# A decode stage woven into a feed-forward block: a value step of its own, and dense products handed out in halves

## The chip, the cores and the metric

The kernel runs on one core of a Trainium2 chip. The metric is the device time of one execution in microseconds (us); the kernel before was run three times, and the median counts. Beside these there is one profiled execution, whose instructions, waits and transfers can be looked at one by one.

## The reference

One layer of a hybrid decoder serves two groups of tokens with the same weights: a prompt of 512 tokens and a sample group of 8 sequences with 4 new tokens each, whose 4096 past tokens lie in a paged cache. Cut to its skeleton:

```python
h = h + 0.5 * rmsnorm(swiglu(rmsnorm(h, g0), wg[0], wu[0], wd[0]), g1)   # first FFN, 1024 -> 2816 -> 1024
m = mixer(rmsnorm(h, g2), ...)     # 4 HGRN2 heads (gated recurrence) and 4 MLA heads
h = h + rmsnorm(m, g3)
h = h + 0.5 * rmsnorm(swiglu(rmsnorm(h, g4), wg[1], wu[1], wd[1]), g5)   # second FFN

# MLA heads, latent form; for the sample group the keys are the cached ones and the new ones
past_c = cache_kv_latent[page_table].reshape(8, 4096, 256)
past_r = cache_k_rope[page_table].reshape(8, 4096, 64)
s = (einsum('bqhr,bsr->bhqs', q_lat, keys_c) + einsum('bqhd,bsd->bhqs', q_rope, keys_r)) / sqrt(192)
o_lat = einsum('bhqs,bsr->bqhr', softmax(masked(s)), keys_c)
```

All inputs and outputs are float32. Outputs are the new activations, the new latent rows and rotary keys, and the recurrent states.

## The kernel before

The 544 tokens are split in two parts: `a` with 256 prompt tokens and `b` with 256 prompt tokens and the 32 sample tokens. Activations lie transposed, features on the 128 partitions and tokens along the free dimension. A float32 product is made of three products of a high and a low part: `weight` (L214) loads a weight tile by a DMA on SyncE's queue into `wraw` (three buffers), casts it to its high part `wh` on ScalarE (L231) and subtracts for the low part `wl` on VectorE (L232); `gemm` (L243, matmuls recorded at L240) and `gemm_q` (L250, L258) multiply. `gemm_q` is a generator that yields behind every second block of 128 features.

The kernel is written as generators that are advanced in turn, and the order in which they are advanced is the order of priority; a scheduler then orders each engine's instructions, keeping to that order as far as its own estimate finds operands ready. So the source gives the order of the work nearly, not to the instruction.

The change is about the decode stage, which lies between the attention over the prompt and the second FFN of part `b`. Two streams share it:

- **Dense:** `gb = ffn(1, 5, (0,), u4, ...)` (L979), the second FFN of part `a`. Its 22 gate-and-up tiles come in chunks of 6, 6, 5 and 5. A tile is 24 products with the gate weights and 24 with the up weights (each 128x128 by 128x256), and behind them on VectorE `sil` times the rms factor (L311), a sigmoid on ScalarE (L287 to L289), two products (L313, L314) and a split into `hha` and `hla` (L154, L155). Behind each chunk stand 8 down columns of 18 or 15 products, added up in `ma` (L329, L331). A tile is one step of the generator, a down column too: 54 steps.
- **Decode:** `decode()` (L1131). The 8 sequences' caches are worked on as 16 halves. For each half `gather` (L1041) fetches two blocks of latent rows (1 MB each) and two of rotary keys by indirect DMAs on GpSimd's queue; the latent blocks go to six slots in turn (`ulb`, `uhb`, `ha`, `hb`, `mb`, `q0`), so that a gathering waits for the value products of three halves earlier. `turn` (L1060) transposes the rows to `kh` on VectorE (L1065, L1066; two buffers, so that it waits for the scores of the half before). `score` (L1069) makes 80 small matmuls of 64x32 weights (L1078), in two bursts of 40, and takes their maxima (`mxd`, `mxh`, L1085 to L1087). `peak` (L1089) spreads the maximum over the partitions with TensorE (L1091) and VectorE (L1093, L1096). `weigh` (L1098) takes exponentials on ScalarE (L1101). `place` (L1103) transposes them and copies them to `pbuf` on VectorE and ScalarE (L1105, L1109). `value` (L1111) makes 16 matmuls of 128x32 weights by 256 columns (L1117), and for every second half `gathered` (L1123) turns the sum (L1128, L1129).

`decode()` counts steps of a third of a half. With `at(k)` for the half that began k halves ago, a third with r = 0 is two steps: the first score burst, then the second burst together with the value products of the half before and the gather of a new half. r = 1 is one step, peak and the turning of the next half; r = 2 is one step, gathered and weigh, and place goes with the step after it. That is 79 steps in all. The loop that advances the two streams keeps them in proportion:

```python
na, nb = NS + (NS + 2) // 3, int((22 + 32) * DRATE)     # 79 decode steps, 43 dense steps
ia, ib = 1, 0
while ia < na:
    if ia * nb <= ib * na:
        next(ga, None)        # a decode step
        next(gn, None)        # scores of the new tokens, a few steps
        ia += 1
    else:
        next(gb, None)        # a dense step
        ib += 1
```

`decode_end` (L1170) combines the parts (`pb`, L1183). What is left of `gb` is handed out by `fill` (L1301) while the output projection and the second FFN of part `b` begin: `FILL` gives the numbers of steps.

Of the kernel before, what the change touches and what calls it, by code (L numbers as in the profile page):

```python
# [49 lines left out]
W0 = 0  # L50
JOBS = (0, 1, 2, 6, 7, 8, 3, 4, 5)
CQ, NST = (0, 0, 0, 3, 1), 3
FILL = (4, (7, 8, 9), (1, 2, 3, 4), 4)
PTB, PEB, QNB = 2, 3, 1
LEP, LXP, EB, XB = (), (), 2, 2
PAT = (2, 2, 2, 2, 2, 2, 2, 2, 2, 2, 1, 1, 1, 2, 3, 2)
PATL = (2, 2, 1, 1, 2, 1, 2, 1, 2, 2, 1, 1, 1, 2, 2, 1)
NW, WX = 2, 2
DRATE = 0.8
KHB = 2  # L60
LEVELS = (64, 32, 16, 8, 4, 2, 1)

# [37 lines left out]
def hybrid_step_kernel(  # L100
# [27 lines left out]
    def ps(name, tag="ps"):  # L128
        return pp.tile([P, 512], F32, name=name, tag=tag, bufs=NPS[tag])
# [30 lines left out]
    def sumsq(srcs, eng=None):  # L160
        n = srcs[0].shape[-1]
        acc = tmp("ssq", n)
        for k, s in enumerate(srcs):
            if k == 0:
                nc.scalar.activation(acc, s, AF.Square)
            else:
                q = tmp("sq1", n)
                nc.scalar.activation(q, s, AF.Square)
                (eng or nc.vector).tensor_tensor(acc, acc, q, op=ALU.add)
        return allsum(acc)  # L170
# [7 lines left out]
    def rstd(out, ss, n, r=None):  # L178
        t = tmp("rs_t", out.shape[-1])
        if r is None:  # L180
            nc.scalar.activation(t, ss, AF.Ln, scale=1.0 / n, bias=epst)
            nc.scalar.activation(out, t, AF.Exp, scale=-0.5)
        else:
            nc.vector.tensor_tensor(t, r, r, op=ALU.mult)
            nc.vector.scalar_tensor_tensor(t, ss, 1.0 / n, t, op0=ALU.mult, op1=ALU.mult)
            nc.scalar.activation(t, t, AF.Ln, scale=1.0, bias=epst)
            nc.scalar.activation(t, t, AF.Exp, scale=-0.5)
            nc.vector.tensor_tensor(out, t, r, op=ALU.mult)
# [19 lines left out]
    def rstd_u(u, x):  # L208
        rstd(u[2], sumsq([h[x][:, k] for k in range(KD)]), D)
# [25 lines left out]
    def mm3(out, pairs):  # L235
        n = 0
        last = 3 * len(pairs) - 1
        for (ah, al), (bh, bl) in pairs:
            for a, b in ((ah, bh), (ah, bl), (al, bh)):
                nc.tensor.matmul(out, a, b, start=n == 0, stop=n == last)  # L240
                n += 1

    def gemm(wt, act_):  # L243
        wh, wl, kt = wt
        acc = ps("acc", "acc")
        n = act_[0].shape[-1]
        mm3(acc[:, :n], [((wh[:, k], wl[:, k]), (act_[0][:, k], act_[1][:, k])) for k in range(kt)])
        return acc[:, :n]

    def gemm_q(wt, act_):  # L250
        wh, wl, kt = wt
        acc = ps("acc", "acc")
        n = act_[0].shape[-1]
        for k in range(kt):
            if k and k % 2 == 0:
                yield
            for i, (a, b) in enumerate(((wh, act_[0]), (wh, act_[1]), (wl, act_[0]))):
                nc.tensor.matmul(acc[:, :n], a[:, k], b[:, k], start=k + i == 0, stop=k == kt - 1 and i == 2)  # L258
        return acc[:, :n]
# [28 lines left out]
        nc.scalar.activation(out, out, AF.Ln, bias=ones[:, :1])  # L288
        nc.scalar.activation(out, out, AF.Exp, scale=-1.0)  # L289

    def ffn(i, n_post, xs, u, nxt=None, mid=None, late=None, fin=None, pre=()):
        pool = cur[-1]
        yield
        r2 = {x: u[x][2] for x in xs}
        mT = {x: actslot("m", x) for x in xs}
        ends = []
        for c, (f0, nf) in enumerate(FCH[i]):
            hh = {x: mk([P, FCH[i][0][1], HS[x]], F32R, "hh" + "ab"[x], pool=pool) for x in xs}
            hl = {x: mk([P, FCH[i][0][1], HS[x]], F32R, "hl" + "ab"[x], pool=pool) for x in xs}
            for j in range(nf):  # L300
                f = f0 + j
                wg_ = (w0 or [weight([wcols(w_g[i], 0, KD, f * P)], KD)]).pop(0)
                ga = {x: gemm(wg_, u[x]) for x in xs}
                wu_ = (w0 or [weight([wcols(w_u[i], 0, KD, f * P)], KD)]).pop(0)
                up = {x: gemm(wu_, u[x]) for x in xs}
                if late and f == 0:
                    late()
                for x in xs:
                    s = tmp("sil", HS[x], 3, pool)
                    t = tmp("sit", HS[x], 2, pool)  # L310
                    nc.vector.tensor_tensor(s, ga[x], r2[x], op=ALU.mult)  # L311
                    sigmoid(t, s)
                    nc.vector.tensor_tensor(s, s, t, op=ALU.mult)  # L313
                    nc.vector.tensor_tensor(s, s, up[x], op=ALU.mult)  # L314
                    split(hh[x][:, j], hl[x][:, j], s)
                yield
            last = c == len(FCH[i]) - 1
            if fin and c == BEG:
                fin.begin(u[xs[0]][2])
            if last:  # L320
                sacc = {x: tmp("ssm" + "ab"[x], HS[x], 1, pool) for x in xs}
            groups = [(d,) for d in range(KD)] if not last or len(xs) == 1 else [(d,) for d in range(KD - STAG)] + [tuple(range(KD - STAG, KD))]
            for grp in groups:
                wts = {d: pre.pop(0) if pre else weight([wcols(w_d[i], f0, nf, d * P)], nf, len(grp) > 1) for d in grp}
                for x in xs:
                    for d in grp:
                        acc = gemm(wts[d], (hh[x], hl[x]))
                        if c == 0:
                            nc.scalar.copy(mT[x][:, d], acc)  # L329
                        else:  # L330
                            nc.vector.tensor_tensor(mT[x][:, d], mT[x][:, d], acc, op=ALU.add)  # L331
                        if last:
                            sq = scale_sq(sacc[x], mT[x], d, gq, n_post, bool(fin) and d == KD - 1)
                        if last and fin and d >= LAG:
                            fin.column(mT[x], d - LAG)
                    if last and grp is groups[-1] and fin:
                        for d in range(KD - LAG, KD):
                            fin.column(mT[x], d)
                        fin.end(sacc[x], sq)
                    elif last and grp is groups[-1]:  # L340
                        ends.append(post(x, mT[x], sacc[x], u[x][2], nxt))
                        next(ends[-1])
                yield
        if mid:
            mid()
        for p in ends:
            for _ in p:
                pass
# [100 lines left out]
    u4 = {}  # L449
# [43 lines left out]
    with scope("mix") as mx_:  # L493
# [234 lines left out]
        with scope("hg"):  # L728
# [9 lines left out]
            for hd in range(NH):  # L738
                nx = hs_[hd + 1][0]() if hd + 1 < NH else some(CQ[hd])
                step = 0  # L740
# [235 lines left out]
    ffa = ExitStack()  # L976
    wx.append(ffa.enter_context(scope("ffa")))
    seam = []
    gb = ffn(1, 5, (0,), u4, late=lambda: rstd_u(u4[0], 0), pre=seam)  # L979
    next(gb)  # L980

    with scope("dec"):
# [48 lines left out]
        NS = 3 * NH2 + 11  # L1031
# [99 lines left out]
        def decode():  # L1131
            H = {}
            for t in range(NS):
                n, r = divmod(t, 3)

                def at(k):
                    return H.get(n - k)

                if n < NH2 and r == 0:
                    H[n] = Half(n)  # L1140
                if r == 0:
                    if at(2):
                        at(2).score(range(5))
                    if n < 3 and at(0):
                        at(0).gather()
                    yield
                    if at(2):
                        at(2).score(range(5, 10))
                    if at(3):
                        at(3).value(H.get(n - 4))  # L1150
                    if n >= 3 and at(0):
                        at(0).gather()
                    yield
                elif r == 1:
                    if at(2):
                        at(2).peak()
                    if at(1):
                        at(1).turn()
                    yield
                else:  # L1160
                    if at(3):
                        at(3).gathered()
                    if at(2):
                        at(2).weigh()
                    yield
                    if at(2):
                        at(2).place()
                H.pop(n - 5, None)
# [36 lines left out]

        ga, gn = decode(), decode_new()
        next(ga)
        na, nb = NS + (NS + 2) // 3, int((22 + 32) * DRATE)
        ia, ib = 1, 0
        while ia < na:  # L1210
            if ia * nb <= ib * na:
# [82 lines left out]
    with scope("fin"):  # L1294
# [22 lines left out]
        next(gp)  # L1317
        fill(FILL[0])
        hm = homes()
        f0, nf = FCH[1][-1]  # L1320
        for d, _ in enumerate(gp):
            if d in FILL[1]:
                fill(1)
            if d in FILL[2]:
                seam.append(weight([wcols(w_d[1], f0, nf, (len(seam) + 1) * P)], nf, home=next(hm)))
        fill(FILL[3])
        next(gB)
# [53 lines left out]
```

## Time and profile before

| | |
|---|---|
| three runs | 1341.04, 1342.49, 1344.46 us, median 1342.49 |
| profiled execution | 1339.38 us, span of its instructions 1337.6 us |
| mean granted TensorE clock | 0.991 |
| instructions | 29702 |
| read from and written to HBM | 181.48 MB and 9.67 MB, 143 GB/s over the span |

The profiled execution's own time is 1.8 us more than the span of its instructions. In the rows that follow, times are microseconds from the span's start; `PE` is TensorE's matmuls and `PEld` its weight loads, `DVE` VectorE, `ACT` ScalarE, `POOL` GpSimd, `SP` SyncE; L1078 is a line of the kernel; `out<-in` names the tiles, with buffer numbers left out; `x48` counts instructions, and a float32 matmul of the source is two rows in the trace. A matmul's duration is modelled and overlaps the next one's, so that the distance between starts tells more than the busy time. A chain of waits goes back from the last instruction, at each step to what released it; "issue" in it is time in which an engine waited for nothing that the profile shows.

### The profile page before, as it was taken

To read this page: it belongs to the slowest core of one execution; us is meant where nothing else is said; L and a number is where in the kernel's file an instruction comes from. 1 tells how busy PE (TensorE), PEld (TensorE's weight loads), DVE (VectorE), ACT (ScalarE), POOL (GpSimd) and SP (SyncE) were. 2 spreads that over 40 slices of the span, in tenths; PEclk is the share of its full clock that TensorE was granted. 3 is DMA by queue.
4 is the path that set the end of the run, shared out by engine and by line. 5 is a ranking of instruction groups with operands and counts; after the bars stand their busy time and mean duration, and the time that the engine had idled before them with its cause. 6 is when DMAs were issued, how large, how long until landed. Compare 5 with 4: busy or idle time off the path is not lost.

```text
span 1337.6 us, 29702 instructions
## 1 busy us (share of the span) xinstructions
PE 1292.3 (97%) x12316; PEld 1221.4 (91%) x12316; DVE 899.3 (67%) x1778; ACT 703.0 (53%) x1430; POOL 75.1 (6%) x79
## 2 busy tenths in 40 slices
PE   7999999999999999999999889999899999999997
PEld 6999999999999999999897787886788999999996
DVE  7553244444458788775867678998888868566664
ACT  6543244224456745454748654653455677554454
POOL 0000000000000000000000212322310000000000
PEclk9999999999999999999999989999999999999998
DMA  6233323232344222233232866977868555556452
GB/s 194 84 87 88 90 85 91 81 97 80 89 117 149 87 64 82 80 82 108 76 101 70 301 200 208 321 258 259 279 212 290 163 151 161 172 157 178 142 168 69
DMA packets 280309, 193.08 MB, mean 144 GB/s; under 512 B 12525, under 2 KB 271054, under 8 KB 275310
## 3 DMA queue, kind: packets, MB, share of 16 engines
q1 hardware_dynamic: 271968, 148.14, 37.9%
q0 software_dynamic: 7168, 41.95, 8.3%
q8 instruction: 97, 1.59, 0.5%
q10 hardware_dynamic: 1038, 1.09, 0.3%
q14 instruction: 38, 0.31, 0.1%
HBM read 181.48 MB, written 9.67 MB: 143 GB/s over the span
## 4 chain that ended last, share of the span: by engine, by line
PE 79%; DVE 11%; ACT 4%; DMA 4%; issue 2%; ACTq 0%; SPq 0%; DVEq 0%
PE acc L240 57%; PE acc L258 9%; DVE kh L1065 3%; DVE wl L232 2%; PE s L1078 2%; PE pa L643 2%; ACT wh L231 1%; DMA wraw<-w_u 1%; PE s L881 1%; PE o L1117 1%; PE pr L175 1%; DMA wraw<-w_g 1%; ACT pbuf L1109 1%; PE zx L544 1%; PE pS L716 1%
## 5 line engine op out<-in xcount | busy, mean ns | idle before, releaser
L231 ACT CAST wh<-wraw 128x1024 fp32r<-128x1024 f32 (+3 forms) x255 | 248.7, 977 | 339.7 <-PE acc L240 273.6
L232 DVE TENSOR_TENSOR wl<-wraw,wh 128x1024 fp32r<-128x1024 f32 (+3 forms) x255 | 288.6, 1133 | 141.3 <-ACT wh L231 140.8
L240 PE MATMUL acc<-uhb,wh 128*128 128x288 f32 x768 | 227.3, 296 | 0.8 <-ACT uhb L191 0.8
L240 PE MATMUL acc<-ulb,wh 128*128 128x288 f32 x768 | 227.0, 296 | 0.0
L240 PE MATMUL acc<-uhb,wl 128*128 128x288 f32 x768 | 225.6, 294 | 0.6 <-DVE wl L232 0.6
L240 PE MATMUL acc<-uha,wh 128*128 128x256 f32 x768 | 220.1, 287 | 5.5 <-DVE sil L311 5.3
L240 PE MATMUL acc<-ula,wh 128*128 128x256 f32 x768 | 217.5, 283 | 1.2 <-DVE ula L192 1.2
L240 PE MATMUL acc<-uha,wl 128*128 128x256 f32 x768 | 216.9, 283 | 0.4 <-DVE wl L232 0.2
L240 PEld LDWEIGHTS acc<-uha,wh 128*128 128x128 f32 x768 | 145.7, 190 | 9.5 <-DVE sil L311 5.7
L240 PEld LDWEIGHTS acc<-ula,wh 128*128 128x128 f32 x768 | 145.6, 190 | 1.7 <-DVE ula L192 1.6
L240 PEld LDWEIGHTS acc<-uha,wl 128*128 128x128 f32 x768 | 145.3, 190 | 1.0 <-DVE wl L232 1.0
L240 PEld LDWEIGHTS acc<-uhb,wh 128*128 128x128 f32 x768 | 144.1, 188 | 1.5 <-ACT uhb L191 1.0
L240 PEld LDWEIGHTS acc<-uhb,wl 128*128 128x128 f32 x768 | 144.4, 188 | 0.8 <-DVE wl L232 0.8
L240 PEld LDWEIGHTS acc<-ulb,wh 128*128 128x128 f32 x768 | 144.1, 188 | 0.1
L240 PE MATMUL acc<-hlb,wh 128*128 128x288 f32 x317 | 93.7, 296 | 0.0
L240 PE MATMUL acc<-hhb,wh 128*128 128x288 f32 x317 | 93.7, 297 | 0.0
L240 PE MATMUL acc<-hhb,wl 128*128 128x288 f32 x317 | 92.9, 294 | 0.0
L240 PE MATMUL acc<-hha,wh 128*128 128x256 f32 x297 | 87.0, 293 | 2.7 <-ACT hha L154 2.7
L240 PE MATMUL acc<-hla,wh 128*128 128x256 f32 x297 | 84.3, 284 | 1.1 <-DVE hla L155 1.1
L240 PE MATMUL acc<-hha,wl 128*128 128x256 f32 x297 | 84.3, 284 | 0.0
L314 DVE TENSOR_TENSOR sil<-sil,acc 128x256 f32<-128x256 f32 (+1 forms) x88 | 38.3, 436 | 49.4 <-PE acc L240 47.0
L313 DVE TENSOR_TENSOR sil<-sil,sit 128x256 f32<-128x256 f32 (+1 forms) x88 | 38.5, 440 | 43.2 <-ACT sit L289 42.9
(466 smaller groups left out, 2825.8 us busy)
## 6 DMA issues: line engine op xcount, KB each, us to landing
wraw<-w_g SPq DMA_DIRECT2D x66, 512.0 KB, 4.1
wraw<-w_u SPq DMA_DIRECT2D x66, 512.0 KB, 3.9
wraw<-w_in SPq DMA_DIRECT2D x24, 512.0 KB, 3.9
wraw<-w_d SPq DMA_DIRECT2D x32, 384.0 KB, 3.5
wraw<-w_d SPq DMA_DIRECT2D x32, 320.0 KB, 3.2
wraw<-w_o SPq DMA_DIRECT2D x16, 512.0 KB, 3.7
wraw<-w_d SPq DMA_DIRECT2D x16, 448.0 KB, 3.5
wraw<-w_d SPq DMA_DIRECT2D x8, 512.0 KB, 3.8
```

What stands on the lines that cost most here:

```text
L175: nc.tensor.matmul(pr[:, :n], ones, acc, start=True, stop=True)
L231: nc.scalar.copy(wh[:, :kt], w[:, :kt])
L232: nc.vector.tensor_tensor(wl[:, :kt], w[:, :kt], f32(wh[:, :kt]), op=ALU.subtract)
L240: nc.tensor.matmul(out, a, b, start=n == 0, stop=n == last)
L258: nc.tensor.matmul(acc[:, :n], a[:, k], b[:, k], start=k + i == 0, stop=k == kt - 1 and i == 2)
L313: nc.vector.tensor_tensor(s, s, t, op=ALU.mult)
L314: nc.vector.tensor_tensor(s, s, up[x], op=ALU.mult)
L544: nc.tensor.matmul(z, w[a][:, k], U[1][b][:, k], start=k + n == 0, stop=k == KD - 1 and n == 2)
L643: nc.tensor.matmul(pa[:, c * 64 : (c + 1) * 64].rearrange("p (n m) -> p n m", m=m), kx[:, cs], up(qx[:, cs]), start=True, stop=True)
L716: nc.tensor.matmul(pS, ks, vb.rearrange("p b d -> p (b d)"), start=True, stop=True)
L1065: nc.vector.transpose(kh[:, a : a + 4, :8].rearrange("p a j k -> p a (j k)"), self.craw[g][:, a : a + 4])
L1078: nc.tensor.matmul(self.s[r][c * 32 : c * 32 + 32, :P], q[rs, j], kh, start=j == 0, stop=j == 9, skip_group_check=True)
```

## The change

The second score burst's step is split: the value products and the late gathers get a step of their own behind it, so a half has five steps where it had four, and decoding 99 where it had 79. `ffn` gets a mode `fine`, used for `gb`: a gate-and-up tile is no longer one step but four, a pause in the middle of the gate products, one between gate and up, one in the middle of the up products and one at the tile's end. A down column stays one step, so that there are 120 dense steps. The loop's proportion is 101 dense to 99 decode steps, and `FILL` hands out 13 steps first where it handed out 4.

```diff
@@ -50,13 +50,13 @@
 W0 = 0
 JOBS = (0, 1, 2, 6, 7, 8, 3, 4, 5)
 CQ, NST = (0, 0, 0, 3, 1), 3
-FILL = (4, (7, 8, 9), (1, 2, 3, 4), 4)
+FILL = (13, (7, 8, 9), (1, 2, 3, 4), 4)
 PTB, PEB, QNB = 2, 3, 1
 LEP, LXP, EB, XB = (), (), 2, 2
 PAT = (2, 2, 2, 2, 2, 2, 2, 2, 2, 2, 1, 1, 1, 2, 3, 2)
 PATL = (2, 2, 1, 1, 2, 1, 2, 1, 2, 2, 1, 1, 1, 2, 2, 1)
 NW, WX = 2, 2
-DRATE = 0.8
+NDEC = 101
 KHB = 2
 LEVELS = (64, 32, 16, 8, 4, 2, 1)
 
@@ -247,12 +247,12 @@
         mm3(acc[:, :n], [((wh[:, k], wl[:, k]), (act_[0][:, k], act_[1][:, k])) for k in range(kt)])
         return acc[:, :n]
 
-    def gemm_q(wt, act_):
+    def gemm_q(wt, act_, step=2):
         wh, wl, kt = wt
         acc = ps("acc", "acc")
         n = act_[0].shape[-1]
         for k in range(kt):
-            if k and k % 2 == 0:
+            if k and k % step == 0:
                 yield
             for i, (a, b) in enumerate(((wh, act_[0]), (wh, act_[1]), (wl, act_[0]))):
                 nc.tensor.matmul(acc[:, :n], a[:, k], b[:, k], start=k + i == 0, stop=k == kt - 1 and i == 2)
@@ -288,7 +288,7 @@
         nc.scalar.activation(out, out, AF.Ln, bias=ones[:, :1])
         nc.scalar.activation(out, out, AF.Exp, scale=-1.0)
 
-    def ffn(i, n_post, xs, u, nxt=None, mid=None, late=None, fin=None, pre=()):
+    def ffn(i, n_post, xs, u, nxt=None, mid=None, late=None, fin=None, pre=(), fine=False):
         pool = cur[-1]
         yield
         r2 = {x: u[x][2] for x in xs}
@@ -300,9 +300,14 @@
             for j in range(nf):
                 f = f0 + j
                 wg_ = (w0 or [weight([wcols(w_g[i], 0, KD, f * P)], KD)]).pop(0)
-                ga = {x: gemm(wg_, u[x]) for x in xs}
+                ga, up = {}, {}
+                for x in xs:
+                    ga[x] = (yield from gemm_q(wg_, u[x], 4)) if fine else gemm(wg_, u[x])
+                if fine:
+                    yield
                 wu_ = (w0 or [weight([wcols(w_u[i], 0, KD, f * P)], KD)]).pop(0)
-                up = {x: gemm(wu_, u[x]) for x in xs}
+                for x in xs:
+                    up[x] = (yield from gemm_q(wu_, u[x], 4)) if fine else gemm(wu_, u[x])
                 if late and f == 0:
                     late()
                 for x in xs:
@@ -976,7 +981,7 @@
     ffa = ExitStack()
     wx.append(ffa.enter_context(scope("ffa")))
     seam = []
-    gb = ffn(1, 5, (0,), u4, late=lambda: rstd_u(u4[0], 0), pre=seam)
+    gb = ffn(1, 5, (0,), u4, late=lambda: rstd_u(u4[0], 0), pre=seam, fine=True)
     next(gb)
 
     with scope("dec"):
@@ -1146,6 +1151,7 @@
                     yield
                     if at(2):
                         at(2).score(range(5, 10))
+                    yield
                     if at(3):
                         at(3).value(H.get(n - 4))
                     if n >= 3 and at(0):
@@ -1205,7 +1211,7 @@
 
         ga, gn = decode(), decode_new()
         next(ga)
-        na, nb = NS + (NS + 2) // 3, int((22 + 32) * DRATE)
+        na, nb = NS + 2 * ((NS + 2) // 3), NDEC
         ia, ib = 1, 0
         while ia < na:
             if ia * nb <= ib * na:
```

## Prediction

> **What bounds the kernel now.** I read the page first, the busy time by stretches next, then the chain of waits and the waits inside the decode stage, and last the groups of VectorE's instructions. From the page:
>
> ```profile
> PE 1292.3 (97%) x12316; PEld 1221.4 (91%) x12316; DVE 899.3 (67%) x1778; ACT 703.0 (53%) x1430; POOL 75.1 (6%) x79
> PE 79%; DVE 11%; ACT 4%; DMA 4%; issue 2%; ACTq 0%; SPq 0%; DVEq 0%
> ```
>
> TensorE is busy for 97% of the span, but only 79% of the chain that ended last is TensorE's; VectorE has 11% of it. The change touches the decode stage alone, so I cut that out: from the first gate products of the second FFN to the first score burst, from there to the last score burst, and to the end of decoding.
>
> ```profile
> core 0: us, PE busy (x) PEld busy (x) DVE busy (x) ACT busy (x) POOL busy (x), PEclk, DMA share, GB/s
> 760.00:799.40 39.40, 33.58 (x254) 32.30 (x252) 31.60 (x57) 22.58 (x44) 4.74 (x4) 0.91 0.73 228
> 799.40:1016.60 217.20, 204.31 (x3846) 172.88 (x3845) 193.78 (x430) 107.86 (x293) 55.98 (x52) 0.98 0.76 259
> 1016.60:1041.00 24.40, 24.22 (x372) 21.53 (x372) 19.94 (x52) 15.71 (x36) 0.00 (x0) 1.00 0.83 258
> ```
>
> In the middle stretch VectorE works 193.78 of 217.20 us, 89%, against 67% over the span: two engines are near their limits here. Matmuls are pipelined, so 204.31 us of busy TensorE says little; what it needs is counted from undisturbed pieces of the chain:
>
> ```profile
> 924.94 0.37 PE o L1128 x4
> 925.31 0.34 PE s L1078 x4
> ...
> 932.57 1.86 PE o L1117 x32
> ...
> 936.77 0.22 PE s L1091 x2
> ...
> 950.35 5.77 PE acc L240 x48
> ...
> 998.34 1.39 PE s L1078 x80
> ...
> 1014.84 1.88 PE acc L240 x15
> 1016.71 2.55 PE s L1078 x160
> ...
> 1041.24 0.43 PE pb L1183 x2
> ```
>
> A gate-and-up tile (48 products) takes 5.77, a down product 1.88 / 15 = 0.125, a half's scores (160 rows, two to a matmul in the code) 2.55, a half's value products 1.86, a peak 0.22, a gathering 0.37 us. From the start of the first score burst (799.4) to that of the last (1016.7) the program's order holds 12 tiles, 363 down products (8 columns of 18, 8 of 18, 5 of 15), 15 scores, 14 values, 15 peaks and 7 gatherings: 69.2 + 45.5 + 38.3 + 26.0 + 3.3 + 2.6 = 184.9 us. It took 217.3, so **TensorE loses 32.4 us**, and VectorE is idle for 23.4. Neither engine's work fills the time: before, a gate-and-up tile is one step and a down column is one step too, so a half meets 96 gate-and-up products in one phase (11.5 us) and 36 down products in the other (4.5 us), while its VectorE work is the same.
>
> Who is waited for, in the same stretch:
>
> ```profile
> PE s L1078 <- issue: 6.9, 6, 2.3
> PE s L1091 <- DVE mxh L1087: 2.2, 4, 1.4
> PE acc L240 <- ACT hha L154: 1.3, 2, 1.0
> PE acc L240 <- DVE hla L155: 1.1, 2, 0.6
> PE o L1117 <- issue: 1.1, 2, 0.8
> ```
>
> The largest item, 6.9 + 1.1 = 8.0 us, has no releaser: TensorE stops in the middle of a burst. The chain shows one stop, and the DMA view of 942.6 to 945.2 us and of the whole span shows what else is going on:
>
> ```profile
> 940.54 2.37 PE s L1078 x108
> 942.91 2.23 issue
> 945.13 0.44 PE s L1078 x11
> ```
>
> ```profile
> q8 instruction: 1, 0.02, 2.3%
> ...
> q8 instruction: 97, 1.59, 0.5%
> ```
>
> One packet of the instruction queue moves in that stop; over the span there are 97 of 16 KB, for 1.59 MB, about one for every 256 of the 24,632 loads and matmuls. A half's scores and values are 384 of these in 4.4 us; a gate-and-up tile is 96 in 5.8. So I read these stops as TensorE running out of fetched instructions in its dense bursts. The Trainium skill, "Runtime: NRT & Kernel Launch", section "Instruction fetch mechanics", has the refill in 16 KiB blocks of 256 instructions, which the packets' size and count bear out, but calls a boundary's cost mostly hidden, and that the 2.23 us stop speaks against.
>
> **The change part by part.** The amount of work is the same: 120 dense steps (88 quarter tiles of 12 products, 32 down columns) stand for 54; decoding takes 100 of them where it took 43, and in both cases that is all but three tiles and eight columns, so `FILL` 13 + 3 + 4 hands out the rest as 4 + 3 + 4 did. GpSimd's instructions keep their order, so the gathers come in the old sequence behind the value products that free their buffers. What moves is how much dense work stands between two decode steps: five pieces for every half, in both phases.
>
> *Start.* The chain there (line numbers are the old kernel's; behind the edits they grow by 5 or 6):
>
> ```profile
> 767.83 7.93 DMA wraw<-w_u
> ...
> 776.92 1.23 DVE wl L232
> 778.15 0.34 DVE sil L311
> 778.49 0.04 issue
> 778.53 8.09 PE acc L240 x48
> ```
>
> In the changed order the first burst stands behind 26 products of this third tile and not behind three tiles. If the late weight (7.93 us) still sets 778.53, it begins at 778.5 + 26 x 0.12 = 781.6 instead of 799.4. It needs the first half's six transposes on VectorE by then, some 6 us; that engine is idle for 7.8 of the 39.4 us, and has three tiles fewer to split by that point. Bounds: 779 (the order no longer puts late weights ahead of `sil`) and 787 (transposes late).
>
> *Between first and last burst.* The new order holds 694 gate-and-up and 333 down products: 14.46 x 5.77 + 333 x 0.125 + 70.2 = 195.2 us of TensorE. For VectorE, rows of 799.4 to 1016.6:
>
> ```profile
> L232 DVE TENSOR_TENSOR wl<-wraw,wh 128x1024 fp32r<-128x1024 f32 (+2 forms) x44 | 46.6, 1060 | 9.1 <-ACT wh L231 8.8
> ...
> L155 DVE TENSOR_TENSOR hla<-sil,hha 128x256 fp32r<-128x256 f32 x13 | 5.4, 417 | 0.1
> ...
> L331 DVE TENSOR_TENSOR ma<-ma,acc 128x256 f32<-128x256 f32 x11 | 4.4, 400 | 1.4 <-PE acc L240 1.4
> ```
>
> A tile costs it two splits (2 x 1.2, by the 1.23 above) and four passes of 0.42, together 4.1; a column one split (about 1.0) and 0.4. That is 2.46 tiles more and 2 columns less: 193.8 + 10.1 - 2.8 = 201 us, or some 200 since consecutive instructions overlap a little. Now the 32.4 us that TensorE loses:
> - Stops in bursts, 8.0: scores come in two bursts of 80 with a dense piece (1.4 to 2.2 us) between, and another piece before the values, so the same instructions are spread over 8 to 9 us and not 4.4. I take half, -4.0; bounds 0 and -8.
> - Short visits: 4 score rows cost 0.34 us against 0.06 at the burst's rate, 0.28 each. The old order has 15 such splinters among down products, the new one 3: -3.4.
> - Peaks: the peak waits for two transposes and the maxima (1.2 + 0.4 + 1.2 + 0.1 = 2.9 us behind the burst); before, 1.86 + 9 x 0.125 = 3.0 us of TensorE cover that in the down phases; now a value burst and two pieces, 4.7 or more: -2.2; bounds 0 and -2.2.
> - A switch more for each of 14 value bursts: nothing in the trace shows it alone; between 0 and the 0.28 of a splinter. I take half, +2.0; ends 0 and +3.9. Splitting the bursts that were whole: 2 x 1.39 against 2.55, 0.23 for each of nine at most: +1, ends 0 and +2.
> - The rest of the losses (last tile of a chunk before its first column, slow clock, accumulators) stays.
>
> The Trainium skill, "TensorEngine Tiling (Array Packing)", section "Key Properties", speaks against the change: "Changing tiling mode (not just tile) drains the TensorE". By that alone the value step adds drains; the splinters' 0.28 us is what this trace shows of them.
>
> Together 32.4 - 9.6 + 3.0 = 25.8, and 195.2 + 25.8 = **221.0 us**. VectorE would be busy for 200 of that, 91%: tight, and why I credit no more.
>
> *Last burst to the end of decoding* (1016.7 to 1041.2, 24.5 us): 30 more down products stand behind it, +3.8: 28.3.
>
> *SyncE's queue.* The fetches of `ha` and `hb` move ahead of two down weights and two tiles' weights: 2.2 MB at the 258 GB/s above, 8.6 us. The seventh column comes some 15 us behind the value product that frees `ha`, so I cost it at nothing; without that cover, up to 5 us.
>
> **Sum:** 781.6 + 221.0 + 28.3 = 1030.9 against 1041.2: 10.3 us less. What follows is unchanged. The profiled execution took 1339.38 (span 1337.6 and 1.8 around it) and would take 1329.1; it lies 3.1 below the median 1342.49, so for the median 1342.5 - 10.3 = **1332.2 us**. A measurement of this kernel can tell about 0.3%, 4 us, from no change.
>
> **Rivals.**
> 1. *VectorE packs fully.* Even pieces leave it idle for 9 us of the stretch: 200 + 9 = 209, 12 less, 1320 us. For it: its waits there are short. Against: it runs in order, and even now at 89%.
> 2. *The stops stay*, because a fetch is not what they wait for, or because it comes late under the gathers anyway. Then the 4.0 go, and with value switches at their upper end another 2: gain 4, 1338 us. For it: the fetch's own packet is in flight for a part of the stop only, and gathers and weights keep coming. The Trainium skill's "Runtime: NRT & Kernel Launch", by which fetches are mostly hidden, would have it so.
> 3. *Slower: ScalarE's queue.* The cast of the next weight waits for TensorE to free its buffer, and the exponentials of a half and its placing queue behind it; more, smaller pieces put a cast ahead of almost every half. Rows of 796 to 1032:
>
> ```profile
> ACT wh L231 <- PE acc L240: 51.5, 21, 5.5
> ...
> ACT q L1101 <- DVE mq L1096: 5.9, 5, 3.1
> ...
> DVE ulb L1105 <- ACT q L1101: 0.9, 1, 0.9
> ```
>
> The casts wait 51.5 us, once for 5.5; VectorE's transpose of the weights and the next burst's PSUM bank wait for those exponentials, and TensorE for both. Against it: VectorE waited for exponentials once, 0.9 us. The earlier start is worth 17.8 and the tail costs 3.8, so the gain is gone if the 15 halves take 231.3, 15.4 each and not 14.7: it decides from 0.7 us a half. At 1.1 us a half, +16 on the stretch, 1348 us.
> 4. *It doesn't do what it says*: a scheduler decides the order. The order shows quarter tiles between nearly all decode steps, so this has 0.02.
>
> **Chances:** forecast (gain 6 to 17) 0.55; rival 1 0.13; rival 2 0.13, half of it over 0.3%; rival 3 0.17, a little of it within 0.3%; rival 4 0.02. Faster 0.55 + 0.13 + 0.06 = 0.74; same 0.07 + 0.02 + 0.02 = 0.11; slower 0.15. The range reaches to rival 1 and past rival 2 to break-even and a little slower, 1319 to 1346.
>
> **What would show it.** Right: the first score burst near 782 us and decoding's end near 1031; the wait of scores for "issue" at half of 6.9 or less; no splinters; VectorE over 90% between the bursts. Wrong: a burst period over 15.4 us, waits of ACT's `q` L1101 or of value products for `pbuf` above 10 us, or the old stops unchanged.

## The result: 1.2% slower, with a decode stage 22 us longer

| | before | changed |
|---|---|---|
| median of 4 runs | 1342.64 us (1341.04 to 1344.46) | 1359.44 us (1355.99 to 1367.99) |
| ratio, 95% interval | | 1.0122 [1.0089, 1.0154] |
| profiled execution (span) | 1339.38 (1337.6) | 1361.77 (1360.0) |
| start of the first score burst, us | 799.4 | 790.8 (forecast 781.6) |
| first to last burst (the stretch), us | 217.2 | 243.9 (forecast 221.0) |
| last burst to the end of decoding (the tail), us | 24.4 | 28.4 (forecast 28.3) |

The forecast was 1332.2 us. Behind decoding both kernels take nearly the same time (296.6 and 296.9 us), so the 22 us lie in the stage: 8.6 us won at the start, 26.7 lost between the bursts, 4.0 lost in the tail.

From the page of the changed kernel, first the busy times, then the shares of the chain, then the granted clock over 40 slices of 34 us:

```profile
PE 1303.8 (96%) x12316; PEld 1231.7 (91%) x12316; DVE 898.1 (66%) x1778; ACT 703.3 (52%) x1430; POOL 71.4 (5%) x79
...
PE 79%; DVE 8%; DMA 5%; ACT 4%; issue 3%; ACTq 0%; SPq 0%; DVEq 0%
```

```profile
PEclk9999999999999999999999789999889999999999
```

The work is the same to the instruction (12316 products), yet TensorE is busy for 11.5 us more, and the clock row dips at its 23rd and 24th digit (the start of the stage) and at its 29th and 30th (952 to 1020 us): some products ran slower. VectorE's share of the chain fell from 11 to 8%, "issue" rose from 2 to 3%. By stretches:

```profile
core 0: us, PE busy (x) PEld busy (x) DVE busy (x) ACT busy (x) POOL busy (x), PEclk, DMA share, GB/s
760.00:790.80 30.80, 25.64 (x152) 24.32 (x152) 23.78 (x48) 17.17 (x36) 4.01 (x4) 0.72 0.59 189
790.80:1034.70 243.90, 220.48 (x3934) 188.00 (x3933) 201.99 (x444) 116.01 (x309) 53.18 (x52) 0.95 0.74 241
1034.70:1063.10 28.40, 28.20 (x403) 25.30 (x402) 21.48 (x53) 16.48 (x37) 0.00 (x0) 1.00 0.85 250
```

VectorE's 201.99 us is the forecast's 200 to 201, but of 243.9 us it is 83%, not 91%: VectorE isn't what fills the time. The waits of that stretch (engine and line, what it waited for: us in all, times, longest):

```profile
PE s L1083 <- issue: 13.1, 6, 3.8
PE s L1096 <- DVE mxh L1092: 4.4, 4, 2.8
PE acc L240 <- ACT hha L154: 2.8, 2, 2.4
PE o L1122 <- ACT pbuf L1114: 1.5, 1, 1.5
PE s L1083 <- ACT q L1106: 1.2, 1, 1.2
```

The stops inside score bursts, which should have halved from 6.9 us, nearly doubled. Two halves of the chain show what they look like (start, duration, what):

```profile
968.32 1.07 PE s L1083 x62
969.39 1.81 issue
971.20 0.62 PE s L1083 x18
971.82 2.38 PE acc L258 x12
...
982.84 1.61 PE acc L258 x12
984.45 1.07 PE s L1083 x62
985.52 3.80 issue
989.32 0.99 PE s L1083 x18
```

The second burst of a half breaks off at row 62 in one half, at row 62 again in the next, then at 58 and 58 (1004.05 and 1020.22 us). Before the stop the piece of 12 takes 1.61 us, behind it 2.38 and more. And nobody else is late: VectorE's transposes for this half had ended (978.93 + 0.70), and VectorE itself then waits for TensorE (its timeline; the bracket is what it waited for):

```profile
978.93 0.70 DVE L1071 STREAM_TRANSPOSE kh<-rraw 128x512 f32<-128x512 f32 x1
...
989.99 1.25 DVE L1070 STREAM_TRANSPOSE kh<-ha 128x1024 f32<-128x1024 f32 x1 [3.53 <-PE s L1083]
```

The DMA queues from 985.3 to 989.5 us (packets, MB, share of the 16 engines) have one instruction packet, in flight from 987.01 to 988.00, among 1543 others:

```profile
q1 hardware_dynamic: 1456, 0.73, 59.2%
q0 software_dynamic: 87, 0.28, 17.2%
q8 instruction: 1, 0.02, 1.5%
```

The packet landed 1.32 us before TensorE went on; at the other four stops between 952 and 1023 us it was 1.32 to 1.44 us.

**Why the same row each time.** The instruction queue brings 16 KB for 256 instructions, so a new block begins every 256 rows (loads, products and a few semaphore instructions). In the gate-and-up phases the new order has a half of about 160 + 24 + 160 + 24 + 64 + 24 + 4 + 24 + 24 + 4 = 512 rows: two score bursts, five pieces, values, peak, and four semaphore instructions behind the values. That is two blocks. Every second half has a gathering of 8 rows more, so that the average is 516. A block boundary that falls into a second burst falls there again in the next half, or 8 rows (4 products) earlier: 62, 62, 58, 58. And there it is worst placed: the block before it is used up in some 3.8 us, by most of a burst, a piece and most of the next burst.

The traces bear this out when TensorE's instructions (`PE` and `PEld` rows, semaphore instructions among them) are counted from the program's first, modulo 256. Between the first and the last burst of the fourteen traces of this case there are 62 stops of 0.4 us or more without a releaser, and 61 of them stand at count 193 or 194, in whatever line that is; in the changed kernel the last five are exactly 512 instructions apart. Most boundaries cost nothing: in the twelve traces with all gathers, 51 of the 81 boundaries whose block had been used up in under 4.5 us have such a stop, and 3 of the 294 others.

**A stop can cost a second time, by the clock.** The busy times and the granted clock (the number behind POOL's) in pairs of windows, one of the changed kernel, then one of the kernel before:

```profile
986.00:989.40 3.40, 0.08 (x8) 0.08 (x16) 0.42 (x1) 0.00 (x1) 0.00 (x0) 1.00 0.73 228
989.40:992.80 3.40, 3.40 (x30) 2.98 (x30) 2.81 (x6) 0.00 (x0) 0.00 (x0) 0.50 0.05 15
```

```profile
943.60:947.00 3.40, 1.87 (x39) 1.10 (x42) 2.42 (x4) 0.00 (x0) 0.00 (x0) 1.00 0.81 254
947.00:950.40 3.40, 3.40 (x35) 3.04 (x27) 3.40 (x7) 1.05 (x2) 2.42 (x3) 1.00 0.70 195
```

Half clock comes in whole windows of 3.41 us that lie on one grid through a run. Between the first and the last burst of the fourteen traces the clock always fell behind a window in which TensorE was busy for 1.51 us or less, and never behind one with more than 1.79; between 1.54 and 1.79 both occur. (Ahead of the first burst one window with 1.85 us was followed by half clock, in the kernel before with halved weights.) So here a stop of 1.9 us or more inside one window made the next run at half clock; the stop of 2.23 us that the prediction showed in the kernel before lay across two windows (1.87 busy in the second) and cost no clock. In the stretch the changed kernel has seven windows at half clock and the end of another, 24.5 us (five behind the stops of 952 to 1023 us), the kernel before two, 6.8. The Trainium skill, "TensorE: Matmul & The Clock Gate", section "What's actually happening", has this window as free-running and 3413 ns long; the grid agrees. It has the clock fall behind an idle window; here one busy for 1.5 us of 3.41 was enough each time.

**At the start** the chain is still that of the late weight:

```profile
774.51 6.56 DMA wraw<-w_u
781.15 1.04 ACT wh L231
...
782.60 0.42 ACT rna L182
...
783.05 0.44 DVE sil L316
...
783.53 1.01 PE acc L258 x3
784.54 1.15 PE o L1029 x4
785.69 5.21 PE acc L258 x23
790.90 1.17 PE s L1083 x49
```

The up weight lands at 781.07 and not at 775.76, ScalarE's `rna` stands behind its cast, and the tile starts at 783.53 and not at 778.53: 5.0 us. Its 26 products in front of the burst run at 0.23 to 0.34 us each and not at 0.12 (the stretch's clock is 0.72): with four other products among them they take 7.4 us and not 3.1, another 4.3. The whole 7.4 us lie in windows at half clock (781.21 to 791.45). Together these are the 9.3 us between 781.6 and 790.9.

### The profile page after: what moved, and what is told of

It is laid out like the page before. It is cut to its first block, busy times and chain, and to the rows that moved or that the text cites. A ratio compares the mean times of both kernels' runs of the same rounds, so it can differ in the third digit from the quotient of the medians.

```text
span 1360.0 us, 29680 instructions
## 1 busy us (share of the span) xinstructions
PE 1303.8 (96%) x12316; PEld 1231.7 (91%) x12316; DVE 898.1 (66%) x1778; ACT 703.3 (52%) x1430; POOL 71.4 (5%) x79
## 4 chain that ended last, share of the span: by engine, by line
PE 79%; DVE 8%; DMA 5%; ACT 4%; issue 3%; ACTq 0%; SPq 0%; DVEq 0%
PE acc L240 52%; PE acc L258 14%; DVE kh L1070 2%; DMA wraw<-w_g 2%; PE s L1083 2%; PE pa L648 2%; PE o L1122 1%; ACT wh L231 1%; DVE wl L232 1%; DMA wraw<-w_u 1%; PE s L886 1%; PE pr L175 1%; PE o L918 1%; PE zx L549 1%; PE pS L721 1%
## 5 line engine op out<-in xcount | busy, mean ns | idle before, releaser
L258 PE MATMUL acc<-uha,wh 128*128 128x256 f32 x528 | 161.4, 306 | 2.6 <-DVE sil L316 2.6
L258 PE MATMUL acc<-ula,wh 128*128 128x256 f32 x528 | 153.4, 291 | 0.0
L258 PE MATMUL acc<-uha,wl 128*128 128x256 f32 x528 | 152.3, 289 | 0.0
L240 PE MATMUL acc<-uha,wh 128*128 128x256 f32 x416 | 118.4, 285 | 1.0 <-DVE sil L316 1.0
L240 PE MATMUL acc<-ula,wh 128*128 128x256 f32 x416 | 117.7, 283 | 0.0
L240 PE MATMUL acc<-uha,wl 128*128 128x256 f32 x416 | 117.4, 283 | 0.1
L258 PEld LDWEIGHTS acc<-uha,wh 128*128 128x128 f32 x528 | 103.6, 197 | 14.6 <-issue 11.4
L258 PEld LDWEIGHTS acc<-ula,wh 128*128 128x128 f32 x528 | 104.0, 197 | 1.2 <-issue 1.0
L258 PEld LDWEIGHTS acc<-uha,wl 128*128 128x128 f32 x528 | 103.7, 197 | 0.2 <-DVE wl L232 0.2
```

## The experiments

My theory behind the result: the new order brings TensorE's stream into step with the blocks of instructions, and fetches come late under the gathers' traffic, so it stops in half after half, and the half clock follows. The counts above show the first part; the runs below try the rest and what a shift of the boundaries does. The rivals: the value step's place, ScalarE's queue (the prediction's third rival), VectorE's queue, or the even pieces themselves. Ratios are to runs of the kernel before on the same chip. A "score row" is a product row; 32 extra products in the code are 64 of them, with their loads 128 rows of the stream.

**1. Shifting the stream by 128 rows at the first half.**

```
 score(), behind self.s = ...
+    if self.n == 0:
+        for e in range(32):          # products into banks that the half then overwrites
+            nc.tensor.matmul(self.s[e % 2][...], q[...], self.kh[...], start=True, stop=True)
```

> The changed kernel with 32 score products (128 rows of TensorE's stream, about 1 us) made once more ahead of the first half's scores and overwritten by them; all else is the same. Theory (late instruction fetch): an instruction packet brings 256 rows, a half in a gate-and-up phase takes 516, so the block boundary falls at nearly the same place in each half, inside the second score burst, after a block that was used up in 3.5 us. Shifted by half a block it falls where a block lasts 5 us or more: the six stops of 2 to 4 us in second bursts behind 950 us shrink below 1 us each, the half-clock windows behind them go, and the time falls by 10 to 20 us, to 1340 to 1350. Rival A (waits of scores on VectorE's transposes that the trace does not show): stops stay, 1360 plus 1. Rival B (ScalarE's queue): same, 1360.

Measured: 1353.66 us, 1.0085 [1.0058, 1.0112], slower than expected. Its waits, and the stops in its chain:

```profile
PE s L1088 <- issue: 10.0, 5, 2.7
```

```profile
850.04 1.24 PE s L1088 x73
851.28 2.17 issue
...
867.27 1.21 PE s L1088 x69
868.48 1.71 issue
...
883.62 1.21 PE s L1088 x68
884.83 2.71 issue
```

The stops did not go, they moved 100 us: from the third gate-and-up phase (952 to 1020 us) into the second, again at nearly one row, a few rows earlier from half to half, as 516 against 512 has it. A shift moves stops, as the theory has it; to lose them it has to be made where no half behind it meets the boundary.

**2. Each part of the change alone.** Quarter tiles without the value step:

```
                         at(2).score(range(5, 10))
-                    yield
                     if at(3):
...
-        na, nb = NS + 2 * ((NS + 2) // 3), NDEC
+        na, nb = NS + (NS + 2) // 3, NDEC
```

> The changed kernel without the value step of its own: value products and late gathers again in the step of the second score burst, 79 decode steps; dense products still in quarter tiles, 101 to 79. Theory (late fetch): a half still takes about 516 rows, and burst and values stand together, so stops stay or grow: 1352 to 1365. Rival C (the value step itself, with its switches between dense and value products, costs the time): back to 1335 to 1345.

The value step with whole tiles:

```
-    gb = ffn(1, 5, ..., pre=seam, fine=True)
+    gb = ffn(1, 5, ..., pre=seam)
-NDEC = 101
+NDEC = 43
-FILL = (13, ...)
+FILL = (4, ...)
```

> The changed kernel with the value step but whole tiles as dense steps (43 to 99), so only the first part of the change. Theory (late fetch, locked in step with the halves by the even pieces): the rows of a half differ from phase to phase, the boundary wanders as before, time near the old one, 1338 to 1348. Rival C (the value step): 1352 or more.

Measured: quarter tiles alone 1345.95 us, 1.0009 [0.9992, 1.0025]; value step alone 1353.01 us, 1.0077 [1.0056, 1.0097]. Both forecasts of my theory missed; the second time is the one that rival C gave. Their waits in the stretch, the quarter tiles first:

```profile
PE s L1096 <- DVE mxh L1092: 8.0, 5, 1.9
PE s L1083 <- issue: 6.0, 4, 2.4
```

```profile
PE s L1083 <- issue: 11.1, 5, 4.3
```

The quarter tiles alone start at 783.2 us and give the 16 us back by 20 more in the stretch and 5 in the tail, with half the changed kernel's stops and twice its waits for the maximum. The value step alone starts as before (801.6), has stops of 11.1 us and 17.1 us at half clock in a stretch of 219.5, and a tail of 28.1. So neither part alone holds the whole loss, and the value step alone, in other company, has nearly the stops of the whole change. Those stops of 0.4 us or more stand at the boundaries of blocks like the others, so they are fetches and not switches between dense and value products. That they are what makes it slower was not tried.

**3. The gathers' traffic.** From the fourth half on no latent blocks are gathered, the tiles of an earlier half are used again (26 of 32 MB are left out; the edit is shortened):

```
+  old = kept.get(self.n % 3)            # from the fourth half on
...
+  craw = old[g]                         # if old
-  nc.gpsimd.indirect_dma_start(craw..., pool_c, off)
+  if not old:
+      nc.gpsimd.indirect_dma_start(craw..., pool_c, off)
```

> The changed kernel that leaves out the gathers of latent rows from the fourth half on (26 of 32 MB); the halves work on the rows of the first three. Instructions of TensorE and VectorE are the same and in nearly the same order. Theory (the fetch is late because its packet stands behind gather traffic): no stop over 1 us in second bursts, at most three half-clock windows in the decode stage, decode stage 20 to 35 us shorter, 1325 to 1340. Rival A or B (VectorE or ScalarE order): stops stay within a few us of 15, 1350 or more.

> The kernel before, leaving out the gathers of latent rows from the fourth half on, as the run of the changed kernel did that took 1335.6. Theory (the stops are late fetches under gather traffic, and without them the even pieces are the better order, as forecast): its 10 us of stops go too, 1328 to 1338, and the changed order stands no worse than it. If the even pieces are worse in themselves: clearly below 1328.

Measured: the changed kernel 1335.56 us (two executions), 0.9937 [0.9913, 0.9962]; the kernel before with the same edit 1336.13, 0.9927 [0.9901, 0.9953]. The stops and the stretch of the first, then of the second:

```profile
PE s L1093 <- issue: 3.1, 4, 1.2
```

```profile
786.70:1007.50 220.80, 208.86 (x3934) 179.28 (x3933) 201.54 (x444) 115.98 (x308) 26.88 (x26) 1.00 0.48 143
```

```profile
PE s L1088 <- issue: 1.6, 3, 0.8
```

```profile
802.40:1013.20 210.80, 201.99 (x3847) 172.45 (x3846) 192.52 (x430) 107.87 (x293) 30.95 (x26) 0.99 0.46 138
```

Same instructions of TensorE in the same order (x3934), 241 GB/s turned into 143: stops 13.1 to 3.1 us, no half clock left in the stretch, which is 220.8 long. With these bytes gone both orders take the same time, so the changed kernel's 17 us all hang on that traffic. It also says that the new order, even pieces and value step together, brings next to nothing in itself: the new order's start is 15.7 us earlier, its stretch 10.0 and its tail 4.0 longer, and beyond what TensorE needs the two orders lose 210.8 - 184.9 = 25.9 and 220.8 - 195.2 = 25.6 us.

**4. The decisive pair: the same place, half a block or a whole one.** The extra products at the eleventh half, ahead of the third gate-and-up phase:

```
+    if self.n == 10:
+        for e in range(32):     # 128 rows; the other kernel: range(64), 256 rows
```

> The changed kernel with the 32 extra score products (128 rows) ahead of the eleventh half, behind the second gate-and-up phase and ahead of the third. The changed kernel stopped in the third such phase (952 to 1020 us), with the shift at the first half it stopped in the second (851 to 920) and not in the third. Theory (block boundary in the second burst): now neither phase stops; unattributed stops of 14.6 us between first and last burst fall under 5, half-clock time there from 24.5 to under 10, time down by 13 to 22 us from the changed kernel's 1359, to 1337 to 1346. Rival D (the stops of the third phase come from how the gathers lie at that time, and the earlier shift only changed the phase by chance): stops stay, 1355 to 1362.

> The same with 64 extra products (256 rows, a whole block) at the same place: twice the extra work, the boundary where the changed kernel has it. Theory: the stops of the third phase are back, 12 us or more unattributed, 1356 to 1364. If extra products as such help, by letting VectorE or a gather catch up: as good as the run with 32 or better.

Measured: 128 rows 1346.35 us, 1.0003 [0.9982, 1.0023]; 256 rows 1361.59, 1.0107 [1.0068, 1.0145]. With 32 products more to do the changed kernel's loss is gone; with 64 at the same place it is back, 15.2 us slower than with 32. Stops and stretch, 128 rows first:

```profile
PE s L1088 <- issue: 2.2, 2, 1.4
```

```profile
784.80:1018.00 233.20, 214.34 (x3998) 182.29 (x3997) 201.28 (x444) 116.11 (x308) 52.45 (x52) 0.99 0.77 252
```

```profile
PE s L1088 <- issue: 15.7, 6, 4.3
```

```profile
786.80:1033.20 246.40, 220.47 (x4065) 188.05 (x4064) 202.21 (x444) 115.97 (x309) 53.35 (x52) 0.96 0.73 239
```

Traffic is nearly alike in both and TensorE's order is the same but for the extra products, and the slower one waits less for the maximum (5.6 us for 7.3) and for the exponentials (1.2 for 4.6); what differs is the stream's place against the blocks, and 64 products more. No theory by ScalarE, VectorE or the value step tells these two apart.

**5. Quarter tiles alone, with the same 128 rows:** the two edits of 2 (first) and 4 (`range(32)`) together.

> Quarter tiles without the value step, with the 32 extra products ahead of the eleventh half. It stopped four times between 950 and 996 us without them, 7.5 us in all. Theory: those go and the half-clock window with them, 8 to 12 us off its 1346, 1334 to 1339, below the kernel before. Rival C (the value step alone makes the difference): no gain, 1344 to 1349.

Measured: 1343.33 us, 0.9987 [0.9967, 1.0007]: the best version with quarter tiles that computes all of it, and not to be told from the kernel before: the gain expected did not come. One stop is left in its profiled execution (1347.48, one of its slower ones), 2.1 us, but the peaks wait 11.0 us in 7 places for the maximum. A piece fewer stands between a half's last score and its peak; that this is why was not tried.

**6. Half of each gate and up weight's bytes** left out, in the 128-row kernel, the kernel before, and the changed kernel (the edit is shortened):

```
-  nc.sync.dma_start(w[:, :kt, ...], s)
+  nc.sync.dma_start(w[:, : kt // 2, ...], s[:, : kt // 2])    # cast and split read it twice
```

> The run with the shift of 128 rows at the eleventh half, which loads only the first half of each gate and up weight tile of the decode stage and uses it twice (0.25 in place of 0.5 MB a tile; casts and splits as large as before). Theory (what is left between this order under gather traffic, 233 us from first to last burst, and without, 221, is weights that land late and hold VectorE's split): VectorE's waits for casts there fall from 17 to under 8 us and the stretch to 221 to 227, the time to 1333 to 1340. Rival (gather traffic costs it in other ways, fetches again or the gathers' own landing): the stretch stays over 230, 1342 or more.

> The kernel before with the same halved loads. Theory: its weights were waited for less (splits waited 8.8 us for casts), so it gains less: 1336 to 1342. If it gains as much or more, the even pieces have no special need of timely weights.

> The changed kernel, not shifted, with the same halved loads. Theory (fetch packets stand behind gather traffic; the block boundary is in the second burst): stops in the third gate-and-up phase stay, 7 us or more unattributed, and it stays 8 to 14 us above the shifted run with the same loads. If weight traffic is what delays fetches: stops go, within 4 us of the shifted run.

Measured: 1340.91 us, 0.9982 [0.9963, 1.0001]; 1337.23, 0.9957 [0.9940, 0.9973]; 1349.67, 1.0038 [1.0011, 1.0065]. The last one's profiled execution (1342.2) is the fastest of its eight, and even that has stops of 8.1 us in 9 places.

Late weights explain little of what the shifted kernel still loses: its stretch falls from 233.2 to 229.7, and the old order gains as much or more. But the unshifted kernel gains most, some 10 us against its 1359.44, and stays 8.8 above the shifted one. So the stops seem to hang on the weights' traffic as well as on the gathers'; how far, its one profiled execution does not tell.

**7. The same 128 rows in the kernel before.**

```
 (kernel before)
+    if self.n == 10:
+        for e in range(32):
```

> The kernel before with 32 extra score products (128 rows) ahead of its eleventh half, whose burst, like the next one, it broke off for 2.2 us near row 300 of 320. There the block boundary before lies in the same burst, so a block lasted 2.4 us; shifted by half a block both neighbours last over 4 us. Theory (late fetch at the block boundary): the stops at 942 and 958 us and the half-clock window behind them go, some 6 us less for 1 us of extra work, unless the shift breaks a later burst in their place: ratio 0.994 to 0.999, and below every full version tried. Rival D (they come from how the gathers lie): both stops stay, ratio 1.000 to 1.002.

Measured: 1348.16 us, 1.0030 [1.0013, 1.0048]; I had expected no stops behind the shift. A miss:

```profile
PE s L1083 <- issue: 6.4, 6, 2.2
```

One stop of the last phase went (958 us), one stayed (947.05), one came (1011.29). All of its stops of 0.4 us or more stand at boundaries again. A whole burst here is 160 products with their loads, 320 rows, more than a block, so every whole burst holds a boundary and no shift can take it out; and the extra rows stand straight ahead of a burst, so that the block in front of the stop at 947.05 was used up in 3.3 us, as it had been without them. That this is why no gain came is argued from the counts, not tried.

## Why the prediction was wrong, point by point

- **The step that failed: "Stops in bursts, 8.0 ... I take half, -4.0; bounds 0 and -8".** They became 13.1 us. The reading was right as far as it went (TensorE out of fetched instructions in dense bursts), but the sum thinned the density and never asked where the 256-row boundaries fall. What the runs showed in its place: the new order's half is two blocks long, so a boundary comes back at the same place of the second burst, behind a block used up in 3.8 us, and under the gathers' traffic the fetch is late there each time. The rows of a half, 512 to 520, could be counted nearly from the rows quoted; a period so near to two blocks was the sign. The bounds left out that stops could grow at all, and the one rival on them ("the stops stay") took them at the old size.
- **"The rest of the losses (... slow clock ...) stays"** failed with it: 24.5 us at half clock, not 6.8, which costs up to half of the 17.7 more, 8.9 us. With 9.1 us of stops above the forecast, 4.4 of peaks and 3.1 of other waits (`hha`, `pbuf`, `q`) that is 25.5, against 48.7 - 25.8 = 22.9 us lost beyond the forecast; the clock's share is an upper bound, and the waits were not taken away singly.
- **Peaks, "-2.2":** 4.4 us of waiting instead of 0, and 7.3 in the 128-row kernel, where most of the stops are gone: a value burst and two pieces do not cover VectorE's maximum.
- **The start, 781.6:** came at 790.8, beyond the upper bound 787. I bounded the transposes; late were the weight's landing (5.0 us with what stands behind its cast) and the products (4.3, at half clock). The row that the prediction quoted there, 8.09 us for 48 products where 5.77 is the undisturbed time, already showed them slow; the sum took the undisturbed 0.12 each.
- **Right:** the amount of work (202.0 us of VectorE for 200 to 201), the tail (+4.0 for +3.8), the count of splinters (15 to 3), and SyncE's moved fetches at nothing: SyncE waited 10.0 us for value products there, and the tail is as forecast. Of the signs of being wrong that it named, the period over 15.4 us came true (243.9 / 15 = 16.3).
- **The stretch's 221.0 and the mechanism of even pieces:** with the gathers left out the new order takes 220.8, so the sum comes out where few stops are left. That is in part luck, since the total holds and not each term: there the old order loses no more than the new one (25.9 and 25.6 us), so what splinters save goes into other waits, such as 3.0 us for exponentials.
- **Rival 3, slower by ScalarE's queue,** named the right sign and the wrong place: `pbuf` 1.5 and `q` 1.2 us, far under the 10 that it needed. Once it is seen, by a late weight and not by a buffer:

```profile
849.17 8.40 DMA wraw<-w_g
857.67 1.05 ACT wh L231
...
859.26 0.25 ACT pbuf L1114
...
859.55 2.20 PE o L1122 x32
```

- **The Trainium skill's "mostly hidden"** ("Runtime: NRT & Kernel Launch", "Instruction fetch mechanics"): hidden it is at 25 of the 31 boundaries in the changed kernel's stretch, and nearly so with 143 GB/s of traffic and not 241 (3.1 us in four stops). At the other six it is not: 13.1 us.

**Open:** the 128-row kernel's stretch is 12.4 us longer than that without the gathers (233.2 and 220.8). Late weights are 3.5 of it; 5.1 are more waits for the maximum, 1.6 more for exponentials, and up to 3.4 the half clock, but those waits were not taken away singly.

## What to carry to other kernels

Where TensorE's stream is dense and regular, count its rows (loads and products) between two repeats: near a multiple of 256 the same place meets the fetch of the next block each time, and it should be a place where a block lasts long. Here half a block of rows more at the right place was worth more than the reordering itself. A stop without a releaser in the chain, with a packet of the instruction queue landing shortly before its end, is a sign of that fetch; that the stops stand at one and the same count modulo 256 settles it. Price such a stop with the clock behind it, and try an order with the traffic left out before believing that the order is what gains.

## What the hardware showed that I had not expected

- A fetch of 16 KB of instructions stopped TensorE for up to 4.3 us under some 240 GB/s of gathers and weights, for 1.2 at most under 143.
- 61 of 62 stops without a releaser stand at the same count of 256 instructions, and nearly all of them behind a block used up in under 4.5 us (with all gathers, 51 of 54).
- 128 more rows at one place made 15.2 us of difference to 256 more at the same place (1346.35 and 1361.59).
- The clock's windows: 3.41 us on one grid through a run; TensorE busy for 1.5 us or less of one, and the next ran at 0.50 each time, where a stop of 2.23 us across two windows cost nothing.
